# Logits of two 64-wide heads: from a stacked hi-and-lo product over 128 rows to three products of 64 rows in halves of the array

## The chip, the cores and the metric

The kernel runs on one core of one Trainium2 chip. The metric is the device time of one execution in microseconds (us). Engines are named as the profile names them: PE (TensorE) for matmuls, PEld for its weight loads, DVE (VectorE), ACT (ScalarE), POOL (GpSimd) and SP (SyncE, which issues DMAs).

## The reference

One decoder block over 512 tokens with 16 meta tokens ahead of them (528 keys), 1024 channels wide. After a layer norm, one projection gives queries, keys, values and gates of two attention branches. The change concerns the logits of both:

```
# differential attention: 8 heads, each with two 64-wide query/key heads c = 0, 1
s = einsum('bhcqd,bhckd->bhcqk', q, k) * 64 ** -0.5 + alibi      # causal
p = softmax(s);  a = p[:, :, 0] - lam * p[:, :, 1];  y_d = a @ v
# stick-breaking attention: 16 heads, 64 wide
z = einsum('bhqd,bhkd->bhqk', q, k) * 64 ** -0.5
log_keep = where(before, log_sigmoid(-z), 0)
a = where(before, exp(log_sigmoid(z) + suffix_sum(log_keep)), 0);  y_s = a @ v
# both: rms norm or none, silu gates, two branch projections, sigmoid merge,
# output projection, residual, layer norm; meta tokens dropped
```

Here lam is a scalar worked out from a small parameter, diff_lambda.

## The kernel before, in words

Products are made in float32r, a rounded form of float32, and each operand that needs the precision is split in two: hi is the value rounded, lo the rest. A product is hi times hi, plus hi times lo and lo times hi.

The opening normalises and transposes the tokens into hTh and hTl (hi and lo, channels on partitions) and makes the first two queries. Its steps stand in a text that the function `order` reads: a letter and digits for each step. H is the cast of half a weight block to hi (`hi`, on ACT), L the subtraction that gives lo (`lo`, on DVE); h, s and l split the tokens, x and y are query matmuls, `meta` and `lm` treat the meta tokens. Until the first unit begins, each engine keeps the written order.

Then come 16 units: 8 of differential attention ("d") and 8 of stick-breaking attention ("s"). A unit holds two 64-wide heads, head 0 on partitions 0 to 63 (LO) and head 1 on 64 to 127 (HI). While unit u computes its attention, PE projects keys and values of unit u+1 (`proj_pos`, two halves of 264 positions) and the query of unit u+2 (`proj_tok`, 512 tokens). `run` interleaves the two when the program is recorded: each projection step adds a number to a counter (0.33 for three matmuls of 264 columns, 0.64 for three of 512), and attention steps are recorded when the counter passes their due time. `spread(gen, t0, dt, count)` gives the steps of a generator due times that are dt apart. After recording, a scheduler orders each engine's instructions by an estimate of when their operands are ready, so what stands in a row on PE can differ from the recorded order.

Logits of a unit go over four blocks of 128 queries, i = 3 down to 0, with NKEY = 528, 400, 272 and 144 keys. Block 3 is done in two pieces of 264 keys. Before the change, the sum over a head's 64 channels is filled up to 128 rows: the query operand A[c] holds hi of head c on its own 64 partitions and lo on the other 64; the key operand `keys[n][c]` has two slices, slice 0 with hi of the keys on both halves, slice 1 with lo on the head's own half and zeros on the other. Two matmuls over 128 rows (one over both slices, where 2 x 144 columns fit a bank) make one head's logits; a helper, `with_lo`, adds the second part in the 144-key case. Each call of `logits` is for one head and takes one bank of the pool `psc`, which has two. `d_scores` then adds the bias and finds the minimum on DVE and takes the exponential on ACT, head by head; `s_scores(unit, c)` runs once for each head, with a mask on DVE, two sigmoids on ACT, a running product and a product on DVE.

`transposed` turns the weights by PE transposes, and `d_values` and `s_values` multiply by the values. After the units come the branch projections, the merge and the output projection.

Of the kernel before, what the change touches and what calls it, by code (L numbers as in the profile page):

```python
# [9 lines left out]
F32 = mybir.dt.float32  # L10
F32R = mybir.dt.float32r
# [5 lines left out]
P = 128  # L17
# [3 lines left out]
M = 16  # L21
# [16 lines left out]
TD = (0.85, 11.0, 14.5)  # L38
# [5 lines left out]
def hybrid_block_kernel(ctx: ExitStack, tc: tile.TileContext, x, meta, emb_g, emb_b, w_in, b_gate,  # L44
# [132 lines left out]
    neg = const.tile([P, M + P], F32, name="neg")  # L177
    g.memset(neg, 0.0)
    g.affine_select(neg, neg, pattern=[[-1, M + P]], compare_op=ALU.is_gt, fill=-1e30, base=M, channel_multiplier=1)
# [49 lines left out]
    HEADS = ((0, LO, HI), (1, HI, LO))  # L229

    def q_hi(n):
        for c, own, _ in HEADS:
            s.activation(A0[n][c][own], pss[n][own], AF.Copy, scale=0.125)

    def q_lo(n):
        for c, own, oth in HEADS:
            a = A0[n][c]
            v.scalar_tensor_tensor(a[oth], pss[n][own], 0.125, a[own].bitcast(F32), op0=ALU.mult, op1=ALU.subtract)
# [72 lines left out]

    steps = dict(a=scaled, d=lambda b, k: scaled(b, k, v), x=lambda b, k: query(0, P * b, P, k),
# [5 lines left out]
    words = dict(hm=lambda: s.copy(hTh[:, :, :M], hF[:, :, :M]), lm=low_meta, norm0=norm0, mnorm=mnorm, mturn=mturn, meta=meta, more=more_banks,  # L318
                 m0=lambda: stats(4, 0), m1=lambda: stats(4, 1), mr=lambda: rstd(4))

    def order(text):
        for step in text.split():
            if step in words:
                words[step]()
            else:
# [5 lines left out]
             a20 a21 a22 a23 a24 a25 a26 a27 x20 x21 x22 x23 N3 t30 t31 t32 t33 x24 x25 x26 x27 mturn  # L331
             a30 a31 a32 a33 a34 a35 a36 a37 x30 x31 x32 x33 x34 x35 x36 x37 y10 y11 y12 y13 y14 y15 y16 y17
             h00 h01 h02 h03 l00 l01 l02 l03 meta h04 h05 h06 h07 l04 l05 l06 l07 hm lm H20 L20 H21 L21
# [12 lines left out]

    lsum = sp.tile([P, 2], F32, name="lsum")
    lscr = sp.tile([P, 64], F32, name="lscr")
    for c in range(2):
        v.tensor_tensor_reduce(lscr, lamb[:, 2 * c, :], lamb[:, 2 * c + 1, :], 1.0, 0.0, ALU.mult, ALU.add,  # L350
                               lsum[:, c:c + 1])
    lexp = sp.tile([P, 2], F32, name="lexp")
    s.activation(lexp, lsum, AF.Exp)
    v.tensor_scalar(nlam, lexp[:, 1:2], lexp[:, 0:1], -LAM_INIT, op0=ALU.subtract, op1=ALU.add)
# [64 lines left out]
    with tc.tile_pool(name="att", bufs=1) as ap:  # L419
# [13 lines left out]

        keys = [[ap.tile([P, 2, L], F32R, name=f"k{c}{n}") for c in range(2)] for n in range(2)]
        for n in range(2):
            for c, oth in ((0, HI), (1, LO)):
                g.memset(keys[n][c][oth, 1, :].bitcast(F32), 0.0)  # L437

        def stage_q(unit, kind, n):

            res = []
            yield from proj_tok(res, "q" + kind, n)
            ps = res[0]
            A = [apool.tile([P, S], F32R, tag=f"A{c}", name=f"A{c}") for c in range(2)]
            for c, own, oth in ((0, LO, HI), (1, HI, LO)):
                s.activation(A[c][own], ps[own], AF.Copy, scale=0.125)
                v.scalar_tensor_tensor(A[c][oth], ps[own], 0.125, A[c][own].bitcast(F32), op0=ALU.mult,
                                       op1=ALU.subtract)
            unit["A"] = A
            yield 0.64  # L450

        def stage_k(unit, kind, n):

            pss = []
            proj = proj_pos(pss, "k" + kind, n)
            K = keys[n % 2]
            for m in range(2):
                while len(pss) == m:
                    yield next(proj, 0.33)
                o = ts(m, H2)  # L460
                for c, own, oth in ((0, LO, HI), (1, HI, LO)):
# [47 lines left out]
        def logits(A, K, i):  # L509

            nk, q = NKEY[i], A[:, ts(i, P)]
            if 2 * nk <= 512:
                ps = psc.tile([P, 512], F32, tag="sc", name="sc")
                pe.matmul(ps[:, :2 * nk].rearrange("p (a n) -> p a n", a=2), q, K[:, :, :nk], start=True, stop=True)  # L514
                yield ps, 0, nk, ps[:, nk:2 * nk]
                return
            for k0, n in [(0, nk)] if nk <= 512 else [(0, H2), (H2, H2)]:
                ps = psc.tile([P, 512], F32, tag="sc", name="sc")
                for m in range(2):
                    pe.matmul(ps[:, :n], q, K[:, m, k0:k0 + n], start=(m == 0), stop=(m == 1))  # L520
                yield ps, k0, n, None

        def with_lo(lo, b, t):

            if lo is None:
                return b
            v.tensor_tensor(t, lo, b, op=ALU.add)
            return t
# [56 lines left out]
        def d_scores(unit, h):  # L585

            K = unit["K"]
            A = unit["A"]
# [14 lines left out]
            for i in reversed(range(NB)):  # L603
                nk = NKEY[i]
                e = [E[c][:, ZOFF[i]:ZOFF[i] + nk] for c in range(2)]
                for c in range(2):
                    m = mn[:, i, c, :]
                    for n, (ps, k0, use, lo) in enumerate(logits(A[c], K[c], i)):
                        if n == 1:
                            yield  # L610
                        b0 = 384 - P * i + k0
                        t = with_lo(lo, bias[:, b0:b0 + use], e[c][:, k0:k0 + use])
                        v.tensor_tensor_reduce(e[c][:, k0:k0 + use], ps[:, :use], t, -1.0, 3e38, ALU.add, ALU.min,
                                               m[:, n:n + 1])
# [3 lines left out]
                    if c == 0:  # L618
                        yield
# [41 lines left out]
        def s_scores(unit, c):  # L661
            K = unit["K"]
            A = unit["A"]
            a = apads[c]
            sg = ap.tile([P, ZW], F32, tag="e0", name="sgm", bufs=2)
            om = ap.tile([P, ZW], F32, tag="e1", name="om", bufs=2)
            for i in reversed(range(NB)):
                nk, z0 = NKEY[i], ZOFF[i]
                for n, (ps, k0, use, lo) in enumerate(logits(A[c], K[c], i)):
                    if n == 1:  # L670
                        yield
                    if k0 + use == nk:
                        w = P if lo is None else use
                        v.tensor_tensor(ps[:, use - w:use], ps[:, use - w:use], with_lo(lo, neg[:, M + P - w:], om[:, ds(z0, w)]),  # L674
                                        op=ALU.add)
                    o = ds(z0 + k0, use)
                    s.activation(om[:, o], ps[:, :use], AF.Sigmoid, scale=-1.0)  # L677
                    s.activation(sg[:, o], ps[:, :use], AF.Sigmoid)
                rev = om[:, z0:z0 + nk][:, ::-1]
                v.tensor_tensor_scan(rev, rev, rev, 1.0, ALU.mult, ALU.min)  # L680
                v.tensor_tensor(a[:, ds(AOFF[i], nk - 1)], sg[:, ds(z0, nk - 1)], om[:, ds(z0 + 1, nk - 1)],
                                op=ALU.mult)
                yield
# [41 lines left out]
        for u, (kind, n) in enumerate(UNITS):  # L725
# [7 lines left out]
            if kind == "d":  # L733
                ta = {}
                steps += spread(d_scores(unit, n), 0.0, TD[0], 10)
# [4 lines left out]
            else:  # L740
# [6 lines left out]
                else:  # L747
                    proj += [gate("d", n, ydT), gate("s", n, ysT)]
                for c in range(2):
                    ta = {}  # L750
                    steps += spread(s_scores(unit, c), 4.4 * c + (2.0 if n == 0 and c == 0 else 0.0), 0.85, 5)
                    parts = transposed(ta, apads[c], c)
                    steps += [(7.0 + 6.5 * c + 0.7 * m, f) for m, f in enumerate(parts)]
                    steps.append((10.5 + 6.5 * c, lambda c=c, ta=ta: s_values(unit, c, n, ta)))
# [123 lines left out]
```

## Time and profile before

| what | value |
|---|---|
| median of 3 runs | 736.61 us (736.59 to 736.7) |
| profiled execution | 736.48 us |
| its span, first to last instruction | 734.7 us |
| mean granted TensorE clock | 0.998 |
| busy PE / PEld / DVE / ACT / POOL | 724.1 / 647.9 / 525.2 / 420.8 / 76.9 us |
| matmuls shown on PE | 4370 |

"Busy" is the time in which at least one instruction of the engine is in flight. Matmuls overlap in the pipeline, so a matmul's shown duration is longer than the distance to the next one's start; that distance is what it costs PE. In a row such as `206.09 0.65 PE L520 MATMUL sc<-k,A 128*128 128x264 f32 x4` the first two numbers are start and length in us, `128*128` is the stationary operand's rows and columns, `128x264` the moving one, and x4 the merged instructions. A row of groups gives, behind its count, busy time in us and the mean of one in ns, then the engine's idle time ahead of it with what released it.

### The profile page before, as it was taken

The page shows a single profiled execution, that of the slowest core. Times are in us where ns is not written, and L with a number is a line of the kernel's source. Part 1 is how long each engine was busy: PE and PEld are TensorE (multiplying, and loading weights), DVE is VectorE, ACT ScalarE, POOL GpSimd, SP SyncE. Part 2 cuts the span into 40 slices and gives each one's busy share as a digit, 9 for nine tenths or more (in the row PEclk, how much of TensorE's full clock was granted, in tenths as well). Part 3 has the DMA queues.
Part 4 walks back from the last instruction along what each step waited for, and adds up shares of the span by engine and source line. Part 5 has one row for each costly group of instructions (what it writes and reads, how often), then busy time and mean ns, then how long its engine had stood idle before and what let it go on. Part 6 is the DMA issues. An engine that isn't in the chain of part 4 may idle for free.

```text
span 734.7 us, 11864 instructions
## 1 busy us (share of the span) xinstructions
PE 724.1 (99%) x4370; PEld 647.9 (88%) x4370; DVE 525.2 (71%) x1166; ACT 420.8 (57%) x1038; POOL 76.9 (10%) x102
## 2 busy tenths in 40 slices
PE   8999999999999999999999999999999999999995
PEld 8899999999999889898989898988888888888885
DVE  6787778877877889696968696969486434326555
ACT  5676778777777867475657575755473323224100
POOL 3210110111000000000000000001001000001101
PEclk9999999999999999999999999999999999999999
DMA  9231311232122122213122213132255333235221
GB/s 270 59 114 59 87 58 58 58 87 58 58 68 77 58 87 58 87 44 94 54 86 70 76 39 89 56 87 87 58 192 152 87 105 96 86 115 173 86 87 57
DMA packets 105340, 63.89 MB, mean 87 GB/s; under 512 B 2065, under 2 KB 100530, under 8 KB 105282
## 3 DMA queue, kind: packets, MB, share of 16 engines
q1 hardware_dynamic: 104098, 58.93, 27.3%
q10 hardware_dynamic: 1184, 4.20, 1.7%
q8 instruction: 34, 0.56, 0.3%
q14 instruction: 24, 0.20, 0.1%
HBM read 61.03 MB, written 2.10 MB: 86 GB/s over the span
## 4 chain that ended last, share of the span: by engine, by line
PE 96%; DVE 2%; ACT 1%; DMA 1%; issue 0%; POOL 0%; DVEq 0%; SPq 0%; ACTq 0%
PE ps L379 25%; PE ps L364 15%; PE ps L365 15%; PE ps L366 15%; PE sc L520 5%; PE t L533 4%; PE pso L820 2%; PE pso L818 2%; PE pso L819 2%; PE t L538 1%; PE bank L263 1%; PE av L694 1%; PE tv L483 1%; PE av L695 1%; PE av L696 1%; PE sc L514 1%
## 5 line engine op out<-in xcount | busy, mean ns | idle before, releaser
L106 DVE TENSOR_TENSOR wl<-raw,wh 128x512 fp32r<-128x512 f32 x188 | 129.3, 717 | 58.1 <-ACT wh L100 57.9
L100 ACT CAST wh<-raw 128x512 fp32r<-128x512 f32 x188 | 107.3, 622 | 110.4 <-PE ps L365 87.0
L379 PE MATMUL ps<-hTh,wh 128*128 128x264 f32 x512 | 147.2, 288 | 0.4 <-ACT wh L100 0.3
L379 PE MATMUL ps<-hTh,wl 128*128 128x264 f32 x512 | 146.5, 286 | 0.2 <-DVE wl L106 0.2
L379 PE MATMUL ps<-hTl,wh 128*128 128x264 f32 x512 | 145.6, 284 | 0.0
L365 PE MATMUL ps<-hTl,wh 128*128 128x512 f32 x368 | 145.0, 394 | 0.0
L364 PE MATMUL ps<-hTh,wh 128*128 128x512 f32 x368 | 144.8, 394 | 0.0
L366 PE MATMUL ps<-hTh,wl 128*128 128x512 f32 x368 | 144.7, 393 | 0.0
L379 PEld LDWEIGHTS ps<-hTh,wh 128*128 128x128 f32 x512 | 96.4, 188 | 1.4 <-ACT wh L100 0.5
L379 PEld LDWEIGHTS ps<-hTh,wl 128*128 128x128 f32 x512 | 96.4, 188 | 0.9 <-DVE wl L106 0.4
L379 PEld LDWEIGHTS ps<-hTl,wh 128*128 128x128 f32 x512 | 96.5, 188 | 0.6
L366 PEld LDWEIGHTS ps<-hTh,wl 128*128 128x128 f32 x368 | 69.2, 188 | 13.5
L364 PEld LDWEIGHTS ps<-hTh,wh 128*128 128x128 f32 x368 | 69.2, 188 | 13.2 <-ACT k L465 0.2
L365 PEld LDWEIGHTS ps<-hTl,wh 128*128 128x128 f32 x368 | 69.1, 188 | 13.1
L544 DVE TENSOR_TENSOR al<-t,ah 128x512 fp32r<-128x512 f32 (+2 forms) x88 | 45.1, 526 | 24.9 <-ACT ah L543 12.4
L680 DVE TENSOR_TENSOR_SCAN om<-om 128x528 f32<-128x528 f32 (+2 forms) x64 | 56.2, 890 | 4.7 <-ACT om L677 4.0
L543 ACT CAST ah<-t 128x512 fp32r<-128x512 f32 (+2 forms) x88 | 39.4, 466 | 28.6 <-PE t L533 16.5
L520 PE MATMUL sc<-k,A 128*128 128x264 f32 (+2 forms) x256 | 55.2, 307 | 0.2 <-POOL k L437 0.2
L520 PEld LDWEIGHTS sc<-k,A 128*128 128x128 f32 x256 | 39.9, 189 | 3.0 <-POOL k L437 0.4
L677 ACT ACTIVATE om<-sc 128x264 f32<-128x264 f32 (+3 forms) x80 | 31.7, 397 | 17.0 <-DVE sc L674 16.0
L533 PE MATMUL t<-idents,apad 128*128 128x128 f32 x240 | 40.7, 272 | 0.0
L777 DVE TENSOR_TENSOR sm<-ps,sm 128x512 f32<-128x512 f32 x16 | 11.0, 690 | 38.6 <-PE ps L366 38.6
(208 smaller groups left out, 1318.1 us busy)
## 6 DMA issues: line engine op xcount, KB each, us to landing
raw<-in_w_in_dram SPq DMA_DIRECT2D x80, 512.0 KB, 3.8
raw<-in_w_br_diff_dram SPq DMA_DIRECT2D x8, 512.0 KB, 3.9
raw<-in_w_br_sb_dram SPq DMA_DIRECT2D x8, 512.0 KB, 3.9
rawo<-in_w_out_dram SPq DMA_DIRECT2D x8, 512.0 KB, 3.8
hr<-in_x_dram ACTq DMA_DIRECT2D x4, 512.0 KB, 6.9
out_dram<-hr SPq DMA_DIRECT2D x8, 256.0 KB, 2.0
xt<-in_x_dram SPq DMA_DIRECT2D x3, 512.0 KB, 8.5
xt<-in_x_dram SPq DMA_DIRECT2D x2, 256.0 KB, 3.2
```

Of the source, the lines that this page charges most:

```text
L100: s.copy(split[n][0][:, o, :], raws[n][:, o, :])
L106: eng.tensor_tensor(wl[:, o, :], raws[n][:, o, :], wh[:, o, :].bitcast(F32), op=ALU.subtract)
L364: pe.matmul(ps, wh[:, k, :], hh[:, k, o:], start=(k == 0), stop=False)
L365: pe.matmul(ps, wh[:, k, :], hl[:, k, o:], start=False, stop=False)
L366: pe.matmul(ps, wl[:, k, :], hh[:, k, o:], start=False, stop=(k == KT - 1))
L379: pe.matmul(ps[:, :H2], a[:, k, :], b[:, k, ts(c, H2)], start=(k == 0 and m == 0), stop=(k == KT - 1 and m == 2))
L520: pe.matmul(ps[:, :n], q, K[:, m, k0:k0 + n], start=(m == 0), stop=(m == 1))
L533: pe.transpose(t[:, o:o + P], a[:, AOFF[i] + j * P:AOFF[i] + (j + 1) * P], ident)
L543: s.copy(h, t[:, o:o + w])
L544: v.tensor_tensor(l, t[:, o:o + w], h.bitcast(F32), op=ALU.subtract)
L677: s.activation(om[:, o], ps[:, :use], AF.Sigmoid, scale=-1.0)
L680: v.tensor_tensor_scan(rev, rev, rev, 1.0, ALU.mult, ALU.min)
```

## The change

Queries and keys are held once, as one hi and one lo tile with both heads on their own partitions. `logits` works on both heads together: for each piece of keys it takes two banks and issues three products for each head (hi hi, lo hi, hi lo), each over the head's 64 rows of the array, recorded alternately for head 0 and head 1. The 144-key case loses its own form and `with_lo` goes. The splits of queries and keys become one cast and one subtraction over 128 partitions. `s_scores` now does both heads; the running products move to a new generator, `s_weights`, one for each head. In `d_scores` both heads' bias steps stand ahead of both exponentials. Due times change with that. In the opening, H20 H21 and L20 L21 move ahead, H30 to L31 move out of `then` to a place behind the first query's split, and the steps of lam (lam0 to lam2) stand among them.

```diff
-TD = (0.85, 11.0, 14.5)
+TD = (1.8, 11.0, 14.5)
...
     def q_hi(n):
-        for c, own, _ in HEADS:
-            s.activation(A0[n][c][own], pss[n][own], AF.Copy, scale=0.125)
+        s.activation(A0[n][0], pss[n], AF.Copy, scale=0.125)
...
-             a20 ... a27 x20 x21 x22 x23 N3 ...
+             a20 ... a27 H20 H21 x20 x21 x22 x23 N3 ...
...
-             h00 ... l03 meta h04 h05 h06 h07 l04 l05 l06 l07 hm lm H20 L20 H21 L21
+             h00 ... l03 L20 L21 meta h04 h05 h06 h07 l04 l05 l06 l07 hm lm lam0
...
+    order("H30 H31 lam1 L30 L31 lam2")
     def then():
-        order("H30 L30 H31 L31")
         q_hi(1)
         q_lo(1)
...
-            K = keys[n % 2]
+            K = [ap.tile([P, L], F32R, tag=f"k{c}", name=f"k{c}", bufs=2) for c in range(2)]
...
-                for c, own, oth in ((0, LO, HI), (1, HI, LO)):
-                    ps = pss[m][own, :H2]
-                    s.copy(K[c][own, 0, o], ps)
-                    v.tensor_tensor(K[c][own, 1, o], ps, K[c][own, 0, o].bitcast(F32), op=ALU.subtract)
-                    s.copy(K[c][oth, 0, o], ps)
+                ps = pss[m][:, :H2]
+                s.copy(K[0][:, o], ps)
+                v.tensor_tensor(K[1][:, o], ps, K[0][:, o].bitcast(F32), op=ALU.subtract)
...
-        def logits(A, K, i):
+        def logits(unit, i):
-            nk, q = NKEY[i], A[:, ts(i, P)]
-            if 2 * nk <= 512:
...
+            nk, q = NKEY[i], ts(i, P)
+            (qh, ql), (kh, kl) = unit["A"], unit["K"]
             for k0, n in [(0, nk)] if nk <= 512 else [(0, H2), (H2, H2)]:
-                ps = psc.tile([P, 512], F32, tag="sc", name="sc")
-                for m in range(2):
-                    pe.matmul(ps[:, :n], q, K[:, m, k0:k0 + n], start=(m == 0), stop=(m == 1))
-                yield ps, k0, n, None
+                pss = [psc.tile([P, 512], F32, tag="sc", name="sc")[:, :n] for c in range(2)]
+                for m, (a, k) in enumerate(((qh, kh), (ql, kh), (qh, kl))):
+                    for ps, own in zip(pss, (LO, HI)):
+                        pe.matmul(ps, a[own, q], k[own, ds(k0, n)], start=(m == 0), stop=(m == 2))
+                yield pss, k0, n
...
-        def s_scores(unit, c):
+        def s_scores(unit):
...
+                    for c, ps in enumerate(pss):
+                        if k0 + use == nk:
+                            v.tensor_tensor(ps[:, use - P:], ps[:, use - P:], neg, op=ALU.add)
+                        s.activation(om[c][:, o], ps, AF.Sigmoid, scale=-1.0)
+                        s.activation(sg[c][:, o], ps, AF.Sigmoid)
+                yield
+
+        def s_weights(unit, c):
+
+            sg, om = (e[c] for e in unit["E"])
...
-                steps += spread(d_scores(unit, n), 0.0, TD[0], 10)
+                steps += spread(d_scores(unit, n), 0.0, TD[0], 5)
...
+                steps += spread(s_scores(unit), 2.0 if n == 0 else 0.0, 1.7, 5)
                 for c in range(2):
-                    steps += spread(s_scores(unit, c), 4.4 * c + (2.0 if n == 0 and c == 0 else 0.0), 0.85, 5)
+                    steps += spread(s_weights(unit, c), 1.75 + 5.25 * c + (2.0 if n == 0 else 0.0), 1.7 - 0.7 * c, 4)
```

What stands in a row on PE in the first unit, at the block of 400 keys, before (ps are projections; sc_689 and sc_700 are banks of head 0 and head 1; k00 and k10 are their keys, A0 and A1 their queries; a matmul is written once with x2 when two alike follow):

```order
L379 MATMUL ps_677<-hTh_144,wl_521 128x264
L520 MATMUL sc_689<-k00_440,A0_171 128x400 x2
L379 MATMUL ps_677<-hTh_144,wh_520 128x264
L379 MATMUL ps_677<-hTl_145,wh_520 128x264
L379 MATMUL ps_677<-hTh_144,wl_521 128x264
```

And after, at the same place (k0 and k1 are now hi and lo of the keys of both heads, A0 and A1 hi and lo of the queries; sc_673 is the bank of head 0):

```order
L382 MATMUL ps_661<-hTh_144,wl_503 128x264
L510 MATMUL sc_673<-k0_444,A0_171 128x400
L510 MATMUL sc_673<-k0_444,A1_172 128x400
L510 MATMUL sc_673<-k1_445,A0_171 128x400
L382 MATMUL ps_661<-hTh_144,wh_502 128x264
```

Three half-array matmuls of one head stand together, with full-array matmuls on both sides; those of head 1 (bank sc_674) follow nine full-array matmuls later. At the beginning of the second unit, on PE as well, the two pieces of head 0 stood in a row before:

```order
L379 MATMUL ps_904<-hTl_145,wh_733 128x264
L379 MATMUL ps_904<-hTh_144,wl_734 128x264
L520 MATMUL sc_921<-k01_442,A0_173 128x264 x2
L520 MATMUL sc_925<-k01_442,A0_173 128x264 x2
L379 MATMUL ps_904<-hTh_144,wh_733 128x264
```

After, the first piece of both heads (banks sc_907 and sc_908) stands there alternately:

```order
L382 MATMUL ps_890<-hTh_144,wl_711 128x264
L510 MATMUL sc_907<-k0_571,A0_173 128x264
L510 MATMUL sc_908<-k0_571,A0_173 128x264
L510 MATMUL sc_907<-k0_571,A1_174 128x264
L510 MATMUL sc_908<-k0_571,A1_174 128x264
L510 MATMUL sc_907<-k1_572,A0_173 128x264
L510 MATMUL sc_908<-k1_572,A0_173 128x264
L382 MATMUL ps_890<-hTh_144,wh_710 128x264
```

So both forms occur. Over the whole program the 480 half-array matmuls stand in 136 unbroken runs, and of the 344 steps from one to the next inside a run 139 change the half.

In the opening, DVE has these in a row before, up to the first key splits and what follows them (L106 is the subtraction `lo`, L274 a token split, L238 the query split, L350 and L354 the steps of lam, L464 a key split):

```order
L106 TENSOR_TENSOR wl<-raw_85,wh 128x512 x2
L274 TENSOR_TENSOR hTl<-hF,hTh 128x256 x8
L238 SCALAR_TENSOR_TENSOR A_171<-bank,A_171 64x512
L238 SCALAR_TENSOR_TENSOR A_172<-bank,A_172 64x512
L350 ISA lscr,lsum<-small 128x64
L350 ISA lsum 128x1
L350 ISA lscr,lsum<-small 128x64
L350 ISA lsum 128x1
L354 TENSOR_SCALAR nlam<-lexp 128x1
L464 TENSOR_TENSOR k_440<-ps,k_440 64x264
L464 TENSOR_TENSOR k_441<-ps,k_441 64x264
L106 TENSOR_TENSOR wl<-raw_85,wh 128x512 x2
```

And after (L270, L234, L315, L322 and L458 are the same steps in that order):

```order
L315 ISA lscr,lsum<-small 128x64
L315 ISA lsum 128x1
L315 ISA lscr,lsum<-small 128x64
L315 ISA lsum 128x1
L270 TENSOR_TENSOR hTl<-hF,hTh 128x256 x8
L234 SCALAR_TENSOR_TENSOR A_172<-bank,A_171 128x512
L106 TENSOR_TENSOR wl<-raw_85,wh 128x512 x2
L322 TENSOR_SCALAR nlam<-lexp 128x1
L458 TENSOR_TENSOR k_445<-ps,k_444 128x264
```

The subtractions of the value weights now stand ahead of the key split, and one query split and one key split stand where two stood.

More of the change, by code (lines that the diff above doesn't have):

```diff
@@ L310, in more_banks, with lam0, lam1, lam2 @@
         tps[1] += banks(SC, SC, TP)
+    lsum = sp.tile([P, 2], F32, name="lsum")
+    lscr = sp.tile([P, 64], F32, name="lscr")
+    lexp = sp.tile([P, 2], F32, name="lexp")
+    def lam0():
+        for c in range(2):
+            v.tensor_tensor_reduce(lscr, lamb[:, 2 * c, :], lamb[:, 2 * c + 1, :], 1.0, 0.0, ALU.mult, ALU.add,
+                                   lsum[:, c:c + 1])
+    def lam1():
+        s.activation(lexp, lsum, AF.Exp)
+    def lam2():
+        v.tensor_scalar(nlam, lexp[:, 1:2], lexp[:, 0:1], -LAM_INIT, op0=ALU.subtract, op1=ALU.add)
     steps = dict(a=scaled, d=lambda b, k: scaled(b, k, v), x=lambda b, k: query(0, P * b, P, k),
@@ L317, in hybrid_block_kernel @@
     steps["H"], steps["L"] = hi, lo
-    words = dict(hm=lambda: s.copy(hTh[:, :, :M], hF[:, :, :M]), lm=low_meta, norm0=norm0, mnorm=mnorm, mturn=mturn, meta=meta, more=more_banks,
+    words = dict(lam0=lam0, lam1=lam1, lam2=lam2, hm=lambda: s.copy(hTh[:, :, :M], hF[:, :, :M]), lm=low_meta, norm0=norm0, mnorm=mnorm, mturn=mturn, meta=meta, more=more_banks,
                  m0=lambda: stats(4, 0), m1=lambda: stats(4, 1), mr=lambda: rstd(4))
@@ L344, in hybrid_block_kernel @@
     s.mul(g08, cols[:, 32:33], 1.0 - LAM_INIT)
[L347 to L354, printed above, removed]
     start.close()
@@ L605, in d_scores @@
                 e = [E[c][:, ZOFF[i]:ZOFF[i] + nk] for c in range(2)]
+                for n, (pss, k0, use) in enumerate(logits(unit, i)):
+                    if n == 1:
+                        yield
+                    for c in range(2):
+                        v.tensor_tensor_reduce(e[c][:, k0:k0 + use], pss[c], bias[:, ds(384 - P * i + k0, use)], -1.0,
+                                               3e38, ALU.add, ALU.min, mn[:, i, c, n:n + 1])
                 for c in range(2):
                     m = mn[:, i, c, :]
[L608 to L614, printed above, removed]
                     if nk > 512:
```

61 lines of the change are left out of this document (17 added, 44 removed).

## Prediction

> **What bounds the kernel now.** I read the page's busy times and chain first, then the busy time by stretch, then the order of time on PE (TensorE).
>
> ```profile
> span 734.7 us, 11864 instructions
> ...
> PE 724.1 (99%) x4370; PEld 647.9 (88%) x4370; DVE 525.2 (71%) x1166; ACT 420.8 (57%) x1038; POOL 76.9 (10%) x102
> ...
> PE 96%; DVE 2%; ACT 1%; DMA 1%; issue 0%; POOL 0%; DVEq 0%; SPq 0%; ACTq 0%
> ```
>
> PE is busy for 99% and holds 96% of the chain that ended last. Since busy shares are averages, I took the stretches of the head units alone:
>
> ```profile
> 40.00:230.00 190.00, 190.00 (x1349) 179.75 (x1348) 151.04 (x467) 143.60 (x379) 21.27 (x18) 1.00 0.25 73
> ...
> 270.00:600.00 330.00, 330.00 (x1925) 291.50 (x1924) 249.01 (x476) 190.93 (x479) 24.81 (x18) 1.00 0.28 84
> ```
>
> The columns are length, then busy time of PE, weight loads, DVE, ACT and POOL, then the granted clock. PE is busy for all of both stretches, at clock 1.00, while DVE idles 39 of 190 us and ACT 139 of 330. So there is no wait on DVE or ACT to be shortened there: whatever the change adds to PE's queue lengthens the run, and what it takes off the other engines earns nothing.
>
> **The logits before.** The rows give counts; the time a matmul holds PE is not its shown duration (pipelined) but the distance from its start to the next start.
>
> ```profile
> L520 PE MATMUL sc<-k,A 128*128 128x264 f32 x128 | 23.7, 286 | 0.2 <-POOL k L437 0.2
> L520 PE MATMUL sc<-k,A 128*128 128x400 f32 x64 | 18.6, 356 | 0.0
> L520 PE MATMUL sc<-k,A 128*128 128x272 f32 x64 | 13.1, 301 | 0.0
> L514 PE MATMUL sc<-k,A 128*128 128x288 f32 x32 | 9.4, 294 | 0.0
> ```
>
> ```profile
> 206.09 0.65 PE L520 MATMUL sc<-k,A 128*128 128x264 f32 x4
> 206.57 0.28 PE L379 MATMUL ps<-hTh,wh 128*128 128x264 f32 x1
> ...
> 460.51 0.53 PE L520 MATMUL sc<-k,A 128*128 128x400 f32 x2
> 460.88 0.28 PE L379 MATMUL ps<-hTh,wl 128*128 128x264 f32 x1
> ...
> 461.37 0.41 PE L520 MATMUL sc<-k,A 128*128 128x272 f32 x2
> 461.62 0.29 PE L379 MATMUL ps<-hTh,wh 128*128 128x264 f32 x1
> ...
> 223.42 0.29 PE L514 MATMUL sc<-k,A 128*128 128x288 f32 x1
> 223.55 0.29 PE L379 MATMUL ps<-hTl,wh 128*128 128x264 f32 x1
> ```
>
> Starts differ by 0.48/4 = 0.120 us for 264 columns, 0.37/2 = 0.185 for 400, 0.25/2 = 0.125 for 272 and 0.13 for 288. All logits take 128 x 0.120 + 64 x 0.185 + 64 x 0.125 + 32 x 0.13 = 15.4 + 11.8 + 8.0 + 4.2 = 39.4 us of PE.
>
> **The logits after.** Per unit and head there are three products where a stack of hi over lo needed two: 12 matmuls of 264, 6 each of 400, 272 and 144, so 192, 96, 96 and 96 over 16 units, 480 where 288 stood. Each uses 64 of 128 rows but streams its full columns. For 144 columns no row exists. The floor under a short matmul is its weight load:
>
> ```profile
> 344.60 0.19 PEld L694 LDWEIGHTS av<-ah,V 128*128 128x128 f32 x1
> 344.71 0.19 PEld L695 LDWEIGHTS av<-al,V 128*128 128x128 f32 x1
> ...
> 344.63 0.43 PE L694 MATMUL av<-ah,V 128*128 128x416 f32 x1
> ```
>
> The second load starts 0.11 after the first, although the matmul that frees its place began at 344.63: loads of 128 columns follow each other at 0.11 at best. I take 0.11 for 144 columns. One after another the new logits hold PE for 192 x 0.120 + 96 x 0.185 + 96 x 0.125 + 96 x 0.11 = 23.0 + 17.8 + 12.0 + 10.6 = 63.4 us, **24.0 more than before**.
>
> Against that stands the overlap of two halves. The source writes the heads alternately, but PE gets them otherwise: in the built order the 480 stand in 136 unbroken runs between full-array matmuls, most of them three of one head (the first place shown of the order), since each head waits for its own bank. Walking the runs and letting a matmul start beside its predecessor only if that uses the other half gives 90 overlapped pairs, not 240: 55 of 264, 20 of 400, 6 of 272, 9 of 144. What a pair saves is not in this trace. If nothing overlaps, 0. If loads keep their 0.11 distance, a pair costs 0.22 at least: 55 x 0.02 + 20 x 0.15 + 6 x 0.03 = 4.3 us. If loads overlap too, the whole second matmul: 55 x 0.12 + 20 x 0.185 + 6 x 0.125 + 9 x 0.11 = 12.0 us. I take **4.3**, since loads 0.11 apart is what the rows show.
>
> **Going into the half array and out.** This is the largest term. The trace has one place where PE goes from 128 rows to fewer and back, the transposes of the 16 meta tokens:
>
> ```profile
> L263 PE MATMUL bank<-hF,raw 128*128 128x128 f32 x64 | 9.4, 277 | 0.1
> ...
> 20.79 0.50 PE L263 MATMUL bank<-hF,raw 128*128 128x128 f32 x3
> 21.21 0.66 PE L297 MATMUL bank<-idents,mn 16*128 16x16 f32 x8
> 21.73 0.21 PE L298 MATMUL bank<-idents,small 17*128 17x17 f32 x1
> 21.87 0.49 PE L263 MATMUL bank<-hF,raw 128*128 128x128 f32 x2
> ...
> 20.79 0.30 PEld L263 LDWEIGHTS bank<-hF,raw 128*128 128x128 f32 x2
> ...
> 21.21 0.57 PEld L297 LDWEIGHTS bank<-idents,mn 16*128 16x128 f32 x8
> ```
>
> Three L263 matmuls take 0.50 and one shows 0.28, so the last starts at 21.01, at 0.11 distance. The next load should start right then; it starts at 21.21, with no wait shown. On the way out, the second L263 starts at 21.87 + 0.49 - 0.28 = 22.08. From 21.01 to 22.08 is 1.07 us. Without interruption it would be 0.11 + 9 x 0.065 (eight steps in 21.21 to 21.73) + 0.11 = 0.80. So one visit to fewer rows costs 0.27 us: PE empties before the new load starts, both times, and the load lies bare. The page "TensorEngine Tiling" of the Trainium skill (Key Properties) says that a change of tiling mode, not of tile, drains TensorE; here it agrees.
>
> For 64 rows the load is of the 0.11 kind, not 0.065, which adds 0.05: 0.32. The ends: 0.27, and twice the way out, 22.08 - 21.73 = 0.35 less 0.065 + 0.11, so 2 x 0.175 = 0.35. A change of columns costs nothing, though:
>
> ```profile
> 241.91 0.39 PE L641 MATMUL av<-ah,V 128*128 128x512 f32 x1
> 242.14 0.27 PE L487 MATMUL t<-idents,vT 128*16 128x128 f32 x1
> 242.17 0.61 PE L520 MATMUL sc<-k,A 128*128 128x264 f32 x3
> ```
>
> The 16-column transpose follows at 0.23, a 512-column distance, and with the third L520 starting at 242.17 + 0.61 - 0.29 = 242.49 the three steps from 242.14 take 0.35, which is 0.11 + 2 x 0.12. By the page's rule this should have drained too, if a 16-column tile is a mode; so the rows decide, and zero stays as a rival. The change narrows rows, so I take 136 x 0.32 = **43.5 us**, between 36.7 and 47.6.
>
> **The rest.** In the opening PE stands idle here:
>
> ```profile
> 33.84 0.39 PE L520 MATMUL sc<-k,A 128*128 128x264 f32 x1 [0.21 <-POOL k L437]
> 34.49 0.39 PE L379 MATMUL ps<-hTh,wh 128*128 128x264 f32 x1 [0.27 <-ACT wh L100]
> 35.22 0.39 PE L379 MATMUL ps<-hTh,wl 128*128 128x264 f32 x1 [0.22 <-DVE wl L106]
> ```
>
> That is 0.70 us. One query split and one key split replace two, and H30/H31 and the lambda steps move ahead of the keys on ACT and DVE; at best all 0.7 goes, at worst L20/L21, now ahead of the meta steps on DVE, delay as much again. I take **-0.7**. No SP order moves. The removed key casts, the query halves, the additions of with_lo, the split of s_scores and s_weights and the exponentials after both heads' minima are costed at nothing: the projection matmuls on PE run beside them all, and if that cover went, the idle 39 us of DVE and 46 of ACT in the first stretch would still take them, since the work shrinks. POOL loses memsets that nothing later waits for.
>
> **Sum.** +24.0 - 4.3 + 43.5 - 0.7 = +62.5 us. The profiled execution took 736.48 us (span 734.7 and 1.8 around it; the median of the runs is 736.61), so 736.5 + 62.5 = 799. Its own range: 24.0 - 12.0 + 36.7 - 0.7 - 4 (144 columns at 0.07 instead of 0.11) = +44 gives 780; 24.0 + 47.6 + 0.7 = +72, and a few us of bank waits, give 812.
>
> **Rivals.** (1) Rows change as free as columns do: +24.0 less 0 to 12.0, less 0.7, so 747 to 760. For it speaks L487, against it the load at 21.21. (2) Faster: each half-array matmul runs beside its twin. That would be 240 pairs: 96 x 0.12 + 48 x (0.185 + 0.125 + 0.11) = 31.7 us, 7.7 less than before; with the opening, 728. "TensorEngine Tiling" (Theoretical Speedup) states up to 2x for a dimension of 64 or less, which would be this case. It decides if 24.0/0.132 = 182 of 240 pairs overlap (a matmul's mean is 63.4/480 = 0.132) and no change of rows costs anything; the order lets 90 meet. (3) A new wait: both banks of the logits go to one pair, so the next pair waits for evacuation, with the projections queued behind it.
>
> ```profile
> L613 DVE CUSTOM_DVE_ANT_0 e<-sc,bias 128x264 f32<-128x264 f32 x32 | 12.6, 428 | 0.8 <-PE sc L520 0.6
> ...
> L677 ACT ACTIVATE om<-sc 128x264 f32<-128x264 f32 x32 | 12.6, 394 | 1.4 <-DVE sc L674 1.0 <-PE sc L520 0.2
> ```
>
> A stick-breaking pair needs four sigmoids, 1.6 us, against steps 1.7 units apart, which is 1.85 us (three matmuls of 0.12 are counted as 0.33). If each of 80 groups waited for one such instruction, 0.41 us, it would be +33 and 832. Against it: a slower PE gives the other engines more time. (4) Costs and gains cancel within 0.2%, about what a measurement of this kernel can tell from no change.
>
> **Chances.** The forecast 0.72, rival 1 0.14, rival 3 0.06, rival 2 0.05, rival 4 0.03. The forecast's own range, 780 to 812, holds about 0.68; with rival 1 the range 748 to 812 holds a little over 0.8. Faster 0.05, same 0.03, slower 0.92.
>
> **What would show it.** The logits should show 480 matmuls with 64 rows. The first load of each run should start some 0.2 us after the matmul before it, and again on the way out. Alternate matmuls starting within less than 0.1 us of each other would show overlap; a 64-row run entered without a gap would refute the main term. PE should stay near 99% busy or show gaps ahead of L510 without a named releaser; waits on DVE or ACT there would be rival 3. ACT and DVE should be busy for less, with no effect on the span.

## The result and the profile after

| | before | after |
|---|---|---|
| median (lowest to highest of 4 runs) | 736.63 us (736.59 to 736.7) | 801.17 us (800.53 to 801.71) |
| span of the profiled execution | 734.7 us | 798.8 us |
| mean granted TensorE clock | 0.998 | 0.996 |

The ratio is 1.0876 (95% interval 1.0863 to 1.0889). The change costs 64.5 us; the forecast was 62.5. The sum was close, but two of its terms were off by about 10 us in opposite directions, and one cost of 5 us was missing.

The page of the changed kernel, with the lines that answer to those of before (span, busy times, chain):

```profile
span 798.8 us, 12022 instructions
...
PE 786.5 (98%) x4562; PEld 666.3 (83%) x4562; DVE 493.1 (62%) x1086; ACT 377.6 (47%) x927; POOL 72.8 (9%) x98
...
PE 98%; DVE 1%; ACT 0%; issue 0%; DVEq 0%; POOL 0%; ACTq 0%; POOLq 0%
```

The busy time by stretch (columns as before):

```profile
40.00:230.00 190.00, 190.00 (x1238) 162.56 (x1239) 119.38 (x372) 101.90 (x276) 16.96 (x12) 1.00 0.21 59
270.00:595.00 325.00, 325.00 (x1913) 272.62 (x1912) 213.94 (x432) 172.09 (x436) 20.67 (x16) 1.00 0.23 66
```

PE is still busy for the whole of both stretches, at full clock. ACT fell from 420.8 to 377.6 us and DVE from 525.2 to 493.1 without any effect on the end, as forecast. But in the first 190 us PE now gets through 1238 matmuls where it did 1349: "busy" does not tell how fast it works.

The groups of the new logits, and of their weight loads:

```profile
L510 PE MATMUL sc<-k,A 64*128 64x264 f32 x192 | 29.7, 322 | 0.0
L510 PE MATMUL sc<-k,A 64*128 64x272 f32 x96 | 19.9, 321 | 0.0
L510 PE MATMUL sc<-k,A 64*128 64x400 f32 x96 | 18.1, 380 | 0.0
L510 PE MATMUL sc<-k,A 64*128 64x144 f32 x96 | 15.0, 291 | 0.0
...
L510 PEld LDWEIGHTS sc<-k,A 64*128 64x128 f32 x480 | 52.7, 185 | 26.5 <-issue 10.0 <-ACT wh L100 1.4 <-ACT sgm L654 0.7
```

The counts are as predicted. The mean of 264 columns is 322 ns instead of 286, and the loads have 26.5 us of idle time ahead of them, 10.0 of it with no releaser that the profile shows ("issue"). A gap without a named releaser ahead of these matmuls was among the signs named; what it is made of, the single visit shows.

**One visit to the half array.** PE and its weight loads around three half-array matmuls of one head:

```profile
111.77 0.39 PE L367 MATMUL ps<-hTh,wh 128*128 128x512 f32 x1
112.00 0.39 PE L368 MATMUL ps<-hTl,wh 128*128 128x512 f32 x1
112.23 0.40 PE L369 MATMUL ps<-hTh,wl 128*128 128x512 f32 x1
112.56 0.56 PE L510 MATMUL sc<-k,A 64*128 64x144 f32 x3
113.05 0.50 PE L367 MATMUL ps<-hTh,wh 128*128 128x512 f32 x1
113.39 0.40 PE L368 MATMUL ps<-hTl,wh 128*128 128x512 f32 x1
```

```profile
112.56 0.41 PEld L510 LDWEIGHTS sc<-k,A 64*128 64x128 f32 x3 [0.36 <-DVE ydT L636]
113.04 0.19 PEld L367 LDWEIGHTS ps<-hTh,wh 128*128 128x128 f32 x1
```

Matmuls of 512 columns start 0.23 apart. Into the half array it is 0.33 (112.23 to 112.56), and on the way out 0.34 (113.05 to 113.39). The load starts only at 112.56, together with its matmul, and on the way out again at 113.04; between full-array matmuls the load starts ahead (the one for the matmul at 113.39 at 113.15). The three matmuls take 0.49, where 3 x 0.11 = 0.33 would do: in the trace they start at 112.56, 112.73 and 112.84, so 0.06 of the 0.16 lies behind the first, whose load was bare, and 0.09 behind the last, ahead of the way out. Above the streams one visit costs 0.10 + 0.16 + 0.11 = 0.37 us. (The 0.36 put down to DVE ydT in the load's row is idle time of the weight loads, not of PE: no wait on PE is shown here, and the run at 92.57 below has the same 0.10 on the way in without a releaser in its row.)

**Two halves side by side.** Three matmuls of one head, then a run with both heads, each with the full-array matmul that follows:

```profile
67.69 0.62 PE L510 MATMUL sc<-k,A 64*128 64x264 f32 x3
68.25 0.39 PE L382 MATMUL ps<-hTl,wh 128*128 128x264 f32 x1
...
92.57 0.63 PE L510 MATMUL sc<-k,A 64*128 64x264 f32 x6
93.13 0.39 PE L382 MATMUL ps<-hTh,wh 128*128 128x264 f32 x1
```

```profile
92.56 0.42 PEld L510 LDWEIGHTS sc<-k,A 64*128 64x128 f32 x6
```

Six take 0.56 us and three take 0.56 us: the second head is free, its loads too (six in 0.42, three above in 0.41). The single starts in the second run are 2 to 3 ns apart in pairs. The prediction had chosen loads that follow each other at 0.11.

**The seam after the last unit.** PE at the end of attention (L677 to L679 are the last products with the values, `ghd` and `gld` are hi and lo of the gated output of the differential branch), then PE's waits of the whole run with the longest first, then a stretch of after and the like stretch of before:

```profile
600.62 0.43 PE L679 MATMUL av<-al,V 128*128 128x512 f32 x1
603.15 0.51 PE L367 MATMUL ps<-ghd,wh 128*128 128x512 f32 x1 [2.10 <-ACT ghd L750]
604.40 0.79 PE L368 MATMUL ps<-gld,wh 128*128 128x512 f32 x1 [0.75 <-DVE gld L751]
604.99 0.63 PE L369 MATMUL ps<-ghd,wl 128*128 128x512 f32 x1
605.42 0.63 PE L367 MATMUL ps<-ghd,wh 128*128 128x512 f32 x1
605.85 0.63 PE L368 MATMUL ps<-gld,wh 128*128 128x512 f32 x1
...
608.12 0.39 PE L368 MATMUL ps<-gld,wh 128*128 128x512 f32 x1
608.35 0.39 PE L369 MATMUL ps<-ghd,wl 128*128 128x512 f32 x1
```

```profile
PE ps L367 <- ACT ghd L750: 2.1, 1, 2.1
...
PE ps L368 <- DVE gld L751: 0.8, 1, 0.8
PE av L678 <- DVE al L527: 0.5, 1, 0.5
```

```profile
604.00:608.00 4.00, 3.60 (x9) 2.88 (x10) 4.00 (x8) 4.00 (x9) 0.00 (x0) 0.57 0.33 106
```

```profile
537.00:541.00 4.00, 4.00 (x19) 3.34 (x18) 4.00 (x8) 4.00 (x9) 0.00 (x0) 1.00 0.23 79
```

PE stands idle for 2.10 + 0.75 + 0.48 = 3.3 us. After that the granted clock is 0.57 over 4 us, and matmuls of 512 columns start 0.43 apart (604.99, 605.42, 605.85) until about 607.9, then 0.23 again (608.12, 608.35). That half clock costs another 1.7 us (about 8 matmuls at 0.20 more), so the seam costs 5.0. The kernel before had 36 projection matmuls on PE behind its last product with the values. They hid this chain: 4.00 of 4.00 busy, clock 1.00. In the new order the last products stand behind the last of those projections. A clock of 0.57 over 4 us is half clock for 3.4 us. The Trainium skill, "TensorE: Matmul & The Clock Gate" (Part 1), gives a window of about 3.4 us after which an idle TensorE runs at half clock. The half clock here lasted as long, but no single wait ahead of it did: the longest was 2.10 us.

### The profile page after: what moved, and what is told of

Its sections match the earlier page's. It is cut to its first block, busy times and chain, and to the rows that moved or that the text cites. A ratio compares the mean times of both kernels' runs of the same rounds, so it can differ in the third digit from the quotient of the medians.

```text
span 798.8 us, 12022 instructions
## 1 busy us (share of the span) xinstructions
PE 786.5 (98%) x4562; PEld 666.3 (83%) x4562; DVE 493.1 (62%) x1086; ACT 377.6 (47%) x927; POOL 72.8 (9%) x98
## 4 chain that ended last, share of the span: by engine, by line
PE 98%; DVE 1%; ACT 0%; issue 0%; DVEq 0%; POOL 0%; ACTq 0%; POOLq 0%
PE ps L382 26%; PE ps L368 14%; PE ps L369 14%; PE ps L367 14%; PE sc L510 9%; PE t L516 3%; PE pso L803 2%; PE pso L802 2%; PE pso L804 2%; PE bank L259 2%; PE t L521 1%; PE av L677 1%; PE tv L476 1%; PE av L678 1%; PE warm L193 1%; PE av L679 1%
## 5 line engine op out<-in xcount | busy, mean ns | idle before, releaser
L106 DVE TENSOR_TENSOR wl<-raw,wh 128x512 fp32r<-128x512 f32 x188 | 129.2, 718 | 106.4 <-ACT wh L100 105.9
L382 PE MATMUL ps<-hTh,wl 128*128 128x264 f32 x512 | 150.2, 293 | 0.0
L382 PE MATMUL ps<-hTh,wh 128*128 128x264 f32 x512 | 150.1, 293 | 0.0
L382 PE MATMUL ps<-hTl,wh 128*128 128x264 f32 x512 | 149.9, 293 | 0.0
L510 PE MATMUL sc<-k,A 64*128 64x264 f32 (+3 forms) x480 | 82.7, 327 | 0.0
L367 PEld LDWEIGHTS ps<-hTh,wh 128*128 128x128 f32 x368 | 69.1, 188 | 14.0
L368 PEld LDWEIGHTS ps<-hTl,wh 128*128 128x128 f32 x368 | 69.1, 188 | 13.9
L510 PEld LDWEIGHTS sc<-k,A 64*128 64x128 f32 x480 | 52.7, 185 | 26.5 <-issue 10.0
L526 ACT CAST ah<-t 128x288 fp32r<-128x288 f32 (+3 forms) x88 | 39.2, 461 | 44.6 <-PE t L516 36.3
L663 DVE TENSOR_TENSOR_SCAN om<-om 128x528 f32<-128x528 f32 (+3 forms) x64 | 55.5, 881 | 5.9 <-ACT om L653 5.8
L597 ACT ACTIVATE e<-e,mn 128x528 f32<-128x528 f32 (+3 forms) x64 | 36.7, 574 | 30.2 <-DVE mn L591 22.6
L591 DVE CUSTOM_DVE_ANT_0 e<-sc,bias 128x264 f32<-128x264 f32 (+3 forms) x80 | 34.0, 435 | 21.6 <-PE sc L510 21.0
```

Source lines behind the costliest of these rows:

```text
L106: eng.tensor_tensor(wl[:, o, :], raws[n][:, o, :], wh[:, o, :].bitcast(F32), op=ALU.subtract)
L367: pe.matmul(ps, wh[:, k, :], hh[:, k, o:], start=(k == 0), stop=False)
L368: pe.matmul(ps, wh[:, k, :], hl[:, k, o:], start=False, stop=False)
L382: pe.matmul(ps[:, :H2], a[:, k, :], b[:, k, ts(c, H2)], start=(k == 0 and m == 0), stop=(k == KT - 1 and m == 2))
L510: pe.matmul(ps, a[own, q], k[own, ds(k0, n)], start=(m == 0), stop=(m == 2))
L526: s.copy(h, t[:, o:o + w])
```

## The experiments

Each kernel was run beside the kernel before on the same chip; ratios have 95% intervals. For the bookkeeping I use PE's time from its first projection matmul to its first branch product, less the idle time shown by name in it: 514.0 us before, 573.9 after, so +59.9.

**Does every pair side by side take the streams away?** In the changed kernel one tile of two banks now serves a pair, so that both heads become ready at once (the pool holds one such tile where it held two single banks).

```diff
...
-                pss = [psc.tile([P, 512], F32, tag="sc", name="sc")[:, :n] for c in range(2)]
+                both = psc.tile([P, 2, 512], F32, tag="sc", name="sc")
+                pss = [both[:, c, :n] for c in range(2)]
```

> The changed kernel, with one tile of two banks for a pair of heads, so that both heads' banks come free together. In the built order the 480 half-array matmuls then stand in 108 runs instead of 136, alternating throughout. Theory (each visit to the half array costs a fixed price of about 0.39 us, and twins overlap fully): 108 x 0.39 = 42.1, the streams 33.1 instead of 39.4, so +35.8, 772 us. Rival A (each half-array matmul is dear by itself, whatever stands next to it): the same 480, so 801. Rival B (waits for the two banks): no bank is left in reserve, so slower than 801, with idle time of PE ahead of the logits.

Measured: 775.93 us (775.35 to 776.26), ratio 1.0537 [1.0521, 1.0553]. All half-array matmuls now stand alternately, in 108 runs instead of 136. With each pair as long as one matmul the streams are 33.1 us, against 39.4 before, so -6.3. The stage took +34.1 us, which leaves 40.4 for 108 visits: 0.374 each. A run of six:

```profile
100.58 0.81 PE L517 MATMUL sc<-k,A 64*128 64x400 f32 x6
101.31 0.39 PE L388 MATMUL ps<-hTh,wh 128*128 128x264 f32 x1
```

0.73 us for six of 400 columns is 3 x 0.185 = 0.56 and 0.17 beyond the streams, as in the run of three. The overlap is whole, and the kernel is still slower than before: the visits alone decide the sign.

**The same products without half rows.** In the changed kernel each head's keys stand in a tile of 128 rows with zeros on the other head's rows; the same 480 matmuls use the full array.

```diff
...
-                        pe.matmul(ps, a[own, q], k[own, ds(k0, n)], start=(m == 0), stop=(m == 2))
+                        pe.matmul(ps, a[:, q], k[c][:, ds(k0, n)], start=(m == 0), stop=(m == 2))
```

> The changed kernel, with the same 480 products over all 128 rows: the key tiles are held for each head, with zeros on the other head's half. Theory (the half array's visits cost, less the overlap): no visits, no overlap, 480 matmuls one after another, 63.0 - 39.4 = +23.6, so 760 us, with every matmul 0.11 to 0.18 after the one before. Rival A (the number of matmuls or a wait for evacuation is what cost 64 us): about 801. Rival C (zero-padded rows are no dearer and only the count of columns matters): the same 760, so this run does not separate it.

Measured: 765.51 us (764.85 to 765.89), ratio 1.0395 [1.038, 1.0411]. The groups are of the same counts, but with shorter means for the short forms:

```profile
L517 PE MATMUL sc<-k,A 128*128 128x272 f32 x96 | 17.3, 289 | 0.0
L517 PE MATMUL sc<-k,A 128*128 128x144 f32 x96 | 14.9, 258 | 0.0
```

The stage took +24.0 us, as forecast for 480 streams in a row. The rest of the 29.2 is the same seam, here 6.5 us (3.0 of waits and 6.8 at half clock), less what the opening gained ahead of the stage and in its waits, about 1. A further 1.1 us of the opening's gain falls inside the stage (see the opening below), so the streams alone took about 25. So going from two products to three costs 24 to 25 us if nothing overlaps, and leaving half rows out makes the changed kernel 35.7 us faster.

**One visit by itself.** The kernel before, with one 64-row matmul of 128 columns added at the head of each of 62 projections and branch products (its result is overwritten), and the same with 128 rows.

```diff
+            if k == 0:
+                pe.matmul(ps[:, :P], onesm[LO], onesm[LO], start=True, stop=True)
```

> The kernel before, with one matmul of 64 rows and 128 columns (a constant tile by itself, overwritten by the first product that follows) at the head of each of 62 projections and branch products. Theory: a lone visit costs 0.4 to 0.5 us beside the matmul itself, so 62 x 0.55 = +34, 771 us. Rival (rows change freely): 62 x 0.11 = +7, 743 us.

```diff
+            if k == 0:
+                pe.matmul(ps[:, :P], onesm, onesm, start=True, stop=True)
```

> As the run with 62 lone matmuls of 64 rows, but over all 128 rows. Both theories: 62 x 0.11 = +7, 743 us. It is the control: the difference between the two runs, divided by 62, is the price of a visit.

Measured: 765.14 us (764.93 to 765.67), ratio 1.0392 [1.0377, 1.0408], with 64 rows; 745.93 us (745.84 to 746.1), ratio 1.0131 [1.0114, 1.0148], with 128 rows. The lone visit on PE:

```profile
54.76 0.28 PE L381 MATMUL ps<-hTl,wh 128*128 128x264 f32 x1
54.88 0.28 PE L381 MATMUL ps<-hTh,wl 128*128 128x264 f32 x1
55.09 0.32 PE L363 MATMUL ps<-onesm 64*128 64x128 f32 x1
55.35 0.40 PE L516 MATMUL sc<-k,A 128*128 128x288 f32 x1
55.58 0.40 PE L366 MATMUL ps<-hTh,wh 128*128 128x512 f32 x1
```

The distances are 0.21 where a 264-column matmul takes 0.12, then 0.26, then 0.23 where 288 columns take 0.13: 0.45 us added in all, the matmul included. 62 x 0.45 = 27.9 is nearly the whole +28.8. With 128 rows each matmul adds 0.12 to 0.14. The two kernels differ in rows alone, by 19.2 / 62 = 0.31 us (0.31 to 0.33 by the rows). I had expected some 6 us more for the 64-row kernel: a lone visit is a little cheaper than one of three or six matmuls. The rival, by which rows change free, is refuted.

**Columns instead of rows.** The kernel before, with the same 62 matmuls of 128 rows and 64 columns.

```diff
+            if k == 0:
+                pe.matmul(ps[:64, :P], onesm[:, LO], onesm, start=True, stop=True)
```

> The kernel before, with one matmul of 128 rows and 64 columns of the array (128 streamed) at the head of each of the 62 projections and branch products. Theory (only a change of rows empties PE): as the control over the full array, +7 to +10, at most 746 us. Rival (any change of the tile's size empties it): as the run of 64 rows, +29, 765 us.

Measured: 744.08 us (744.0 to 744.16), ratio 1.0101 [1.0087, 1.0115], +7.6 us, which is no more than the 128-column control. Going to 64 columns costs nothing beyond the matmul; going to 64 rows costs a third of a microsecond.

**Must the twins alternate?** In the changed kernel the two loops are swapped: three products of head 0, then three of head 1.

```diff
-                for m, (a, k) in enumerate(((qh, kh), (ql, kh), (qh, kl))):
-                    for ps, own in zip(pss, (LO, HI)):
+                for ps, own in zip(pss, (LO, HI)):
+                    for m, (a, k) in enumerate(((qh, kh), (ql, kh), (qh, kl))):
```

> The changed kernel, with each head's three products issued together, head 0 and then head 1. In the built order the 480 stand in 153 runs, and only 33 steps inside a run change the half. Theory (0.35 us for a visit, overlap of twins nearly whole, as the three runs so far fit): 153 x 0.35 = 53.6, the streams 63.0 less 4.1 instead of 39.4, the opening and the end of the attention as in the changed kernel, +4: in all +78, 814 us. Rival (overlap is worth nothing, and a visit 0.27): 41.3 + 23.6 + 4 = +69, 805 us.

Measured: 810.57 us (809.7 to 811.29), ratio 1.1 [1.0983, 1.1017], between the two expectations. The half-array matmuls now stand in 153 runs. A run that is built as three of head 0 and then three of head 1, with the matmul behind it:

```profile
64.35 0.64 PE L510 MATMUL sc<-k,A 64*128 64x264 f32 x6
64.92 0.39 PE L382 MATMUL ps<-hTh,wh 128*128 128x264 f32 x1
```

In strict order only the third and the fourth could overlap: 0.20 beyond the streams, as in the run of three above, and 5 x 0.12, so 0.80. It took 0.57, as in the alternate order. So the halves go on independently: the single starts stand in pairs, 10 to 15 ns apart, which is the fourth matmul beside the first. Counting for each run only the longer half, the streams are 51.3 us (+11.9); the stage took +69.1, which leaves 57.2 / 153 = 0.374 a visit. In the changed kernel itself the same counting gives 47.4 (+8.0) and (59.9 - 8.0) / 136 = 0.382. Three kernels with 108, 136 and 153 visits agree on a price of 0.37 to 0.38 us. The starts in the traces bear the counting out: leaving out every logit matmul that starts less than 0.03 us behind the one before it, the streams come to 33.3, 47.7 and 51.6 us.

**The opening alone.** The kernel before with nothing but the opening's new order.

```diff
-             h00 ... meta h04 ... l07 hm lm H20 L20 H21 L21
+             h00 ... L20 L21 meta h04 ... l07 hm lm lam0
...
+    order("H30 H31 lam1 L30 L31 lam2")
...
-        order("H30 L30 H31 L31")
```

> The kernel before, with the change's order of the opening alone (H20 H21 and L20 L21 ahead, H30 to L31 out of the callback, the steps of lam among them); logits and splits as before. Theory (the 0.7 us in which PE stood idle ahead of the first logits go, 0.9 with what the run over all rows showed): -0.4 to -0.9, 735.5 to 735.9. Rival (the gain came from the single splits, not from the order): within 0.2 us of before.

Measured: 735.06 us (734.83 to 735.6, 11 runs), against 736.46 (736.12 to 737.72, 15 runs), ratio 0.9981 [0.9972, 0.9989]: 1.4 us faster, and the fastest of all kernels here. Of the gaps behind the first logits one remains:

```profile
33.44 0.39 PE L527 MATMUL sc<-k,A 128*128 128x264 f32 x1 [0.21 <-POOL k L444]
33.67 0.30 PE L386 MATMUL ps<-hTh,wh 128*128 128x264 f32 x1
```

The waits for `wh` (0.27) and `wl` (0.22) are gone, since the splits that kept ACT and DVE from those weights now come earlier. These 0.5 us are not the whole gain, whose interval is about 0.8 to 2.1 us. With 112 projection matmuls, six logit matmuls and two transposes done, the next matmul starts at 43.53 us before and at 42.12 here, and the distance stays near 1.4 to the end of the attention, so the gain is made in the opening. A wait of PE costs more than its idle time: the two logit matmuls at 33.34 and 33.84 us start 0.50 apart before, where 0.12 would do, with 0.21 of it listed as idle. At the same place the full-array kernel starts at 41.34, 2.2 us ahead of before; 0.4 of that is an earlier first projection matmul, which the kernel with 153 visits, with the same opening, does not show; 0.7 are the listed waits, and 1.1 falls inside the stage without being listed. If it does so in the other kernels with the changed opening too, the prices of a visit above are about 0.01 too low. What adds to the 1.4 there was not tried separately.

**The seam, first try.** In the changed kernel the last unit's weights, transposes and values fall due earlier by 2.5 (head 1: 5) of the planner's units.

```diff
+                    e = 2.5 if last else 0.0
...
-                    steps.append((12.5 + 5.0 * c, lambda c=c, ta=ta: s_values(unit, c, n, ta)))
+                    steps.append((12.5 - e + (5.0 - e) * c, lambda c=c, ta=ta: s_values(unit, c, n, ta)))
```

> The changed kernel, with the last unit's running products, transposes and value products due 2.5 units earlier (5 for head 1), so that the casts of its weights stand ahead of the last weight block's cast on ACT. Theory (PE stands idle for 3.4 us at the end of the attention and then runs at half clock for another 3.4): both go, 3.4 + 1.7 = 5.1 less, 796 us. Rival (the wait there is set by something else, or the time is lost again later): 801.

Measured: 800.19 us (800.0 to 800.87), ratio 1.0865 [1.085, 1.088]. The edit did not do what it was meant to. The 0.5 us wait went, but the longest one grew from 2.1 to 2.5 us, and as much half clock followed:

```profile
PE ps L367 <- ACT ghd L751: 2.5, 1, 2.5
...
PE ps L368 <- DVE gld L752: 0.8, 1, 0.8
```

The scheduler still put the last products behind the last projection on PE: recording a step earlier does not move it there. So this run told nothing on the cause, and the dependency was then written by hand.

**The seam, second try.** In the changed kernel 24 projection matmuls of the last merge gate are tied behind the last product with the values.

```diff
+            if (kind, i) == ("ms", 2) and k == 0:
+                tc.add_manual_dep(nc.cur_bb.bb.instructions[-1], state["av"].name, ...,
+                                  reason="cover of the last values")
...
```

> The changed kernel, with the last merge gate's 24 projection matmuls (ms, block 2) held back on PE until the last value product of the attention has been issued, so that they run while ACT and DVE split the attention's output. Theory (the 3.4 us of idle PE at the end of the attention, and the 1.7 us lost in 3.4 us at half clock behind it, come from PE having no projection left there): both go, -5.1, 796 us, with a clock of 1.0 throughout. Rival (the splits of the output or the weight casts behind them are what is late, whatever PE does): the wait moves a few us on, and the time stays at 800 to 801.

Measured: 796.96 us (796.48 to 797.35), ratio 1.0821 [1.0801, 1.084]: 4.2 us less than the changed kernel (3.5 between the two profiled runs). The first branch product now follows a projection matmul without a gap, at full clock:

```profile
602.12 0.39 PE L373 MATMUL ps<-hTh,wl 128*128 128x512 f32 x1
602.34 0.39 PE L367 MATMUL ps<-ghd,wh 128*128 128x512 f32 x1
602.57 0.39 PE L372 MATMUL ps<-gld,wh 128*128 128x512 f32 x1
```

```profile
604.00:608.00 4.00, 4.00 (x19) 3.31 (x18) 4.00 (x7) 4.00 (x9) 0.00 (x0) 1.00 1.02 386
```

```profile
PE t L525 <- DVE al L531: 0.7, 1, 0.7
PE av L678 <- DVE a L551: 0.6, 1, 0.6
PE av L677 <- DVE ysT L687: 0.4, 1, 0.4
```

What is left are 1.7 us of shorter waits ahead of the last products, which the tied matmuls no longer fill, and no half clock follows them. So the cause of the seam is shown: the cover was gone.

## Why the prediction was right in its sum, and where its steps were off

| term | forecast | measured | from |
|---|---|---|---|
| 480 streams in a row, less the overlap | +24.0 - 4.3 = +19.7 | +24 - 16 = +8.0 | the full-array kernel; streams counted by the longer half |
| 136 visits | +43.5 (0.32 each) | +53 (0.39 each) | stage +59.9, and the 1.1 of the opening inside it, less 8.0; 0.37 to 0.38 without the 1.1 |
| seam behind the last unit | nothing | +5.0 | waits 3.3, half clock 1.7; 3.5 to 4.2 recovered |
| opening | -0.7 | -1.8 to -2.2, of it -1.4 by the order alone | the full-array kernel; the opening's order alone |
| sum | +62.5 | +63.8 to +64.2 | measured +64.5 |

That the sum came within 2 us is partly luck: the overlap was 12 us larger than forecast and the visits 9.5 us dearer, and these errors cancel but for 2; the missing seam and the larger gain of the opening make up the rest.

- **What bounds the kernel** was read rightly. PE was the bound before and after; 43 us less on ACT and 32 less on DVE brought nothing.
- **The streams** in a row were right (24.0 against 24 to 25). The step that failed is the choice among the bounds of the overlap: I took 4.3 because the loads of the trace never followed each other faster than 0.11. Those rows were loads of the full array. Loads of two halves go in parallel, which the Trainium skill states in "TensorEngine Tiling (Array Packing)" (Key Properties: tiles execute loads and matmuls in parallel); here six loads took 0.42 where three took 0.41. My upper bound of 12.0 was too low as well, since it counted only neighbours in built order. The halves do not keep that order, so what counts is the longer half of each run, which saves about 16.
- **The visits** were the right mechanism, and the one row of before with a change of rows carried it. The price was mis-sized, 0.32 against 0.38, and lies above the 0.35 that I had as its upper end. Both ends of a visit cost about 0.10 in the start of the next matmul, and inside it another 0.16 to 0.20 goes to the bare first load and to the end of the last matmul. Against the 0.27 of the visit to 16 and 17 rows that is 0.11 more, where I had added 0.05 for the longer load; what makes up the other 0.06 was not tried.
- **The cover.** "The projection matmuls on PE run beside them all" failed in one place. I asked what it would cost if DVE and ACT had less cover in the middle of the run, and not whether the last unit still had projections behind it. The new due times moved the last products behind the last projection, which the built order of PE shows before anything is timed. Idle time of 3.3 us brought half clock on top.
- **The opening** gained more than the 0.7 us of idle time that I had as the most: PE lost more to each wait than the idle time listed for it.
- **The rivals.** Rows that change free: refuted by the 64-row and 128-row controls. Faster through full overlap: its first half is true, and more so than I allowed for (twins that stand in one run overlap), but its second condition, no price for rows, fails; with every pair together the kernel takes 775.93 us. Bank waits: no wait of PE on a logit bank is listed. That columns change free held in the run made for it; the drain that the same section of "TensorEngine Tiling (Array Packing)" states for a change of mode is therefore seen here for rows and not for columns.

## What to carry to other kernels

Two matmuls in the two row halves of the array really take the time of one, but each excursion into half rows among full-array matmuls cost 0.38 us here, as much as three matmuls of 264 columns. With all 240 pairs overlapped the streams save 7.7 us, so by these numbers (an estimate, not run) the packing would pay only in fewer than about 20 visits; collect such work into few long runs or leave it on full rows. And where due times move, look at what stands last on the bounding engine at the end of a stage: a lost cover costs its own wait and then the clock.

## What the runs showed of the hardware that was not expected

- The two row halves proceed independently: a run built as 000111 takes 0.57 us, like 010101 (0.56), where strict order would give 0.80. The Trainium skill, "TensorE: Matmul & The Clock Gate" (Part 3), has matmuls start and end strictly in program order; the measured duration does not fit that for matmuls in different halves. The trace does not name the head in a row, so this rests on the total of the run and the starts in pairs.
- A change to 64 rows costs 0.31 to 0.39 us a visit, while a change to 64 columns costs no more than the matmul of 128 columns (62 of them: +7.6 us against +9.6).
- Idle time of 3.3 us on PE, in three pieces with a little work between, was followed by 3.4 us of half clock; 1.7 us in three pieces was not. In the kernel with alternate pairs, with 3.0 us idle, the half clock lasted twice as long. What decides its length was not tried.
